# Attention of the second layer with plain fp32 products on half arrays, two heads at a time, in a two-layer diffusion backbone on one Trainium2 core

## The chip, the cores and the metric

The kernel runs on one core of a Trainium2 chip. The metric is device time in microseconds for one execution, and the figure quoted is the median of several. PE is the matrix engine TensorE (PEld its weight loads), DVE is VectorE, ACT is ScalarE, POOL is GpSimd and SP is the queue that issues the loads from memory.

## The reference, cut to what matters

The model has two layers over 256 latent tokens (x) and 256 context tokens (c), width 1024. Each layer is a feed-forward network, a token mixer, and a second feed-forward network, each behind a modulated RMS norm. The first layer mixes with latent attention. The second, the last one, mixes with windowed attention (SWA): 16 query heads of 64 in 4 groups, one key and value head per group, and a sink logit per head. Only the latent stream has an output, so only latent queries are needed.

```
q_x, k_x, v_x = project(hx);  q_c, k_c, v_c = project(hc)      # 16 q heads, 4 k and v heads, of 64
q_x_rot, k_x_rot = apply_rope(q_x), apply_rope(k_x)
s_w = where(|kpos - qpos| <= 128, q_rot . k_rot, NEG) * scale  # latent keys: rotated
s_c = q_plain . k_c * scale                                    # context keys: not rotated
p_w, p_c = softmax over [s_w, s_c, sink logit]
out = (p_w . v_x + p_c . v_c) @ w_o
```

## The kernel before

Activations lie transposed: a tile has 128 features in its partitions and 512 columns, 256 latent (X) and 256 context (C). Almost every product is made by `mm3`: both operands are split into a high part (fp32r) and a low part (what is left), and three fp32r matmuls add high·high, high·low and low·high into a bank of PSUM (lines L210, L211 and L212). `split` makes the parts: a cast on ACT (L182) and a subtraction on DVE or POOL (L183). Weights are loaded by SP, 128x1024 at a time, and split in the same way into `whi` and `wlo`.

The order of the instructions on each engine is fixed when the program is built, by a scheduler that may move independent work; the rows under "The change" show that order. Tiles come from rings: 8 banks of PSUM, 46 `r2k` tiles (128x512), 7 `strip`, 6 `tmp`, 4 `big`, 4 `whi` and 4 `wlo`. A new tile waits until the last reader of the one it replaces is done.

`swa` is the function that changes. It works on 8 pairs of heads, m = 0 to 7; here a pair is two neighbouring heads of one group, 128 features of the query projection. Its steps are these:

- `project(m)` multiplies the normed input by a 128-column block of the query weights (24 matmuls). The plain query goes to two tiles, one for each head: `stack` puts the high part of the head's 64 rows in one half of the partitions and the low part in the other half (a cast on ACT, L515, and a subtraction on DVE or POOL, L516, of 64 partitions each). So a product over all 128 partitions takes in high and low of one head at once.
- `rope(m)` rotates: a matmul with a permutation `perm` swaps halves (L497), DVE multiplies by sine and cosine (L499, L501), POOL adds (L502), and `stack` splits the result again, with the subtractions on POOL.
- `keys` and `doubled` do the like for the keys: their high part stands in both halves of one tile and their low part in both halves of another (L521 to L524), for each of the 4 groups.
- `scores(m)` makes four banks, two heads by two blocks of 128 queries, each 128 x 512 keys: four fp32r matmuls of 256 columns (L763 to L766) and one bf16 matmul that adds the mask band (L768).
- `softmax` takes each bank: maximum on DVE (L451, L455), exponential with sum on ACT (L457), then sink and reciprocal (L463, L464, L466) and scaling on DVE (L471) or ACT (L469).
- `turn` transposes the weights (16 transposes on PE, L479) into four banks, each of which `split` turns into two tiles.
- `apply(m)` multiplies by the values: 24 matmuls (8 `mm3` terms) into one bank. The values lie in `big` tiles with zeros between the groups' 64 columns, so that each head adds zeros to the other's 64 output rows. Then a `split`.

`pipeline` runs the steps in rounds: turn(h), project(h+4), scores(h+2), rope(h+3), apply(h). Below, the round of h is the time from the start of turn(h) to the start of turn(h+1) on PE. Ahead of round 0 stand keys, values and the first projections and scores; behind round 7 `closing` multiplies by the output weights `swo`, whose splits the scheduler places partly inside the rounds. The bank ring is passed 11 times a round: four for turn, one for project, four for scores, one for rope and one for apply.

Of the kernel before, what the change touches and what calls it, by code (L numbers as in the profile page):

```python
# [17 lines left out]
P = 128  # L18
# [19 lines left out]
def hybrid_backbone_kernel(ctx, tc, t, out):  # L38
# [9 lines left out]
    def r2k(n=512, parts=P):  # L48
        return ring.tile([parts, n], F32R, tag="r2k", name="r2k", bufs=46)
# [7 lines left out]
    def big():  # L57
        return ring.tile([P, 1152], F32R, tag="big", name="big", bufs=4)
# [120 lines left out]
    def split(hi, lo, src, bias=None, engine=nc.vector):  # L179

        if bias is None:
            nc.scalar.copy(hi, src)  # L182
            return engine.tensor_tensor(lo, src, hi.bitcast(F32), ALU.subtract)  # L183
# [326 lines left out]

    def stack(dst, R, half, engine=nc.vector):

        a = slice(64 * half, 64 * half + 64)
        b = slice(64 - 64 * half, 128 - 64 * half)
        nc.scalar.copy(dst[a], R[a])  # L515
        return engine.tensor_tensor(dst[b], R[a], dst[a].bitcast(F32), ALU.subtract)  # L516
# [189 lines left out]


    def swa(sl, nxt):
        l, hs = sl.l, sl.hs
        K, V, W = [None] * 4, [], {}  # L710
# [23 lines left out]
        ropes = {}  # L734

        def project(m):
            if m < len(sl.lead):
                o = sl.lead[m][1]
            else:
                wt = weight(t["swq"][m], engine=nc.vector if m == 2 else nc.gpsimd)  # L740
                o = bank()
                mm3(o[:, :T], sl.terms(wt, P, X))
            qs = [r2k(), r2k()]
            for i, q in enumerate(qs):
                stack(q[:, C], o[:, :T], i)
            ropes[m] = StackedRope(o[:, :T], [q[:, C] for q in qs]), qs
            return qs

        def rope(m):
            R = strip()  # L750
            rp, qs = ropes.pop(m)
            rp.into(R)
            for i, q in enumerate(qs):
                stack(q[:, X], R, i, nc.gpsimd)

        def scores(m, *qs):
            k = K[m // 2]
            os = []
            for half, q in enumerate(qs):
                for i in range(2):  # L760
                    o = bank()
                    qx, qc = q[:, i * P:(i + 1) * P], q[:, T + i * P:T + (i + 1) * P]
                    nc.tensor.matmul(o[:, X], lhsT=qx, rhs=k[0][:, X], start=True, stop=False)  # L763
                    nc.tensor.matmul(o[:, X], lhsT=qx, rhs=k[1][:, X], start=False, stop=False)
                    nc.tensor.matmul(o[:, C], lhsT=qc, rhs=k[0][:, C], start=False, stop=False)
                    nc.tensor.matmul(o[:, C], lhsT=qc, rhs=k[1][:, C], start=False, stop=False)  # L766
                    far = slice((1 - i) * P, (2 - i) * P)
                    nc.tensor.matmul(o[:, far], lhsT=ident16, rhs=band[:, i, :], start=False, stop=True)  # L768
                    os.append((o, TT))
# [3 lines left out]
            return softmax(os, SWA_SCALE, place, sink[:, heads], minus_sink[:, heads])  # L773

        def turn(*es):
            return [transposed(es[2 * half:2 * half + 2], k0) for half in range(2) for k0 in (0, 2)]
# [12 lines left out]
        kx = [keys(m, 0) for m in range(2)]  # L789
        kropes = [Rope(o) for o in kx]  # L790
        values(0, 2)
        Rs = [tmp() for _ in range(2)]
        for R, rp in zip(Rs, kropes):
            rp.into(R[:, X])
        rope(0)
        rope(1)
        for m, R in enumerate(Rs):
            nc.scalar.copy(R[:, C], keys(m, 1))
        for m, R in enumerate(Rs):
            for i in range(2):  # L800
                kk = (r2k(), r2k())
                doubled(*kk, R, i)
                K[2 * m + i] = kk
# [110 lines left out]
def _layout(x, c, ctx, c_ctx, mod_w, mod_b, norm_g, final_norm_g, ffn_w_in, ffn_w_out, mla_w_down, mla_q_norm,  # L914
# [36 lines left out]
    put("swq", tiles(swa_w_qkv[0][:, :1024], P).reshape(8, P, 1024))  # L951
    put("swk", tiles(swa_w_qkv[0][:, 1024:1280], P).reshape(2, P, 1024))
    put("swv", swa_w_qkv[0][:, 1280:].reshape(2, 4, P, 256).transpose(0, 2, 1, 3).reshape(2, P, 1024))
    put("swo", tiles(swa_w_o[0], P).reshape(KT, P, 1024))
    put("sink", np.broadcast_to(swa_sink[0][None, :], (P, 16)))
# [34 lines left out]
```

## Time and profile before

| what | value |
|---|---|
| median of 3 runs | 1734.75 us (1734.36 to 1736.54) |
| the profiled execution | 1734.44 us, its span 1732.5 us |
| instructions in the span | 24034 |
| PE busy | 1682.6 us (97%) |
| DVE busy | 1065.3 us (61%) |
| ACT busy | 666.9 us (38%) |
| POOL busy | 185.2 us (11%) |
| scores(0) starts on PE | 1400.43 us |
| turn(1) starts | 1433.17 us |
| turn(5) starts | 1477.89 us |

The profiled execution's own time is 1.9 us above its span, and 0.3 us below the median. Busy times of PE are generous, since matmuls overlap in the pipeline and their ends are modelled: two matmuls of 280 ns that start 120 ns apart each count until they end. So the text works with the distances between starts. All times of day are microseconds from the span's start.

### The profile page before, as it was taken

To read this page: it belongs to the slowest core of one execution; us is meant where nothing else is said; L and a number is where in the kernel's file an instruction comes from. 1 tells how busy PE (TensorE), PEld (TensorE's weight loads), DVE (VectorE), ACT (ScalarE), POOL (GpSimd) and SP (SyncE) were. 2 spreads that over 40 slices of the span, in tenths; PEclk is the share of its full clock that TensorE was granted. 3 is DMA by queue.
4 is the path that set the end of the run, shared out by engine and by line. 5 is a ranking of instruction groups with operands and counts; after the bars stand their busy time and mean duration, and the time that the engine had idled before them with its cause. 6 is when DMAs were issued, how large, how long until landed. Compare 5 with 4: busy or idle time off the path is not lost.

```text
span 1732.5 us, 24034 instructions
## 1 busy us (share of the span) xinstructions
PE 1682.6 (97%) x9512; PEld 1440.9 (83%) x9512; DVE 1065.3 (61%) x1592; ACT 666.9 (38%) x1135; POOL 185.2 (11%) x183
## 2 busy tenths in 40 slices
PE   7999999999999999999999999999999988989997
PEld 4688888888788898888888898888888888889997
DVE  4877576645667567856946374635433589755554
ACT  4322222225556352222222352222222577554443
POOL 1000000004132130000000220000000452110001
PEclk9999999999999999999999999999999999999998
DMA  8566355431212136644645254634222221145553
GB/s 331 187 199 195 129 188 189 147 125 64 86 49 72 51 98 203 198 147 156 219 126 172 93 173 160 215 121 161 94 98 92 93 85 46 53 148 182 173 191 99
DMA packets 72831, 242.71 MB, mean 140 GB/s; under 512 B 8848, under 2 KB 10640, under 8 KB 72720
## 3 DMA queue, kind: packets, MB, share of 16 engines
q1 hardware_dynamic: 72720, 241.20, 42.3%
q8 instruction: 74, 1.21, 0.3%
q14 instruction: 37, 0.30, 0.1%
HBM read 240.11 MB, written 1.05 MB: 139 GB/s over the span
## 4 chain that ended last, share of the span: by engine, by line
PE 87%; DVE 5%; issue 2%; ACT 2%; POOL 1%; DMA 1%; SPq 0%; POOLq 0%; ACTq 0%; DVEq 0%
PE bank L210 28%; PE bank L211 28%; PE bank L212 28%; DVE r2k L183 1%; DVE small L451 1%; PE bank L157 1%; DVE wlo L183 1%; DMA r2k<-in_modo 1%; PE bank L479 1%; PE bank L223 0%; POOL wlo L183 0%; PE bank L102 0%; DMA big<-in_win 0%; DVE r2k L294 0%; ACT r2k L182 0%
## 5 line engine op out<-in xcount | busy, mean ns | idle before, releaser
L210 PE MATMUL bank<-r2k,whi 128*128 128x512 f32 (+1 forms) x2610 | 915.2, 352 | 4.0 <-ACT r2k L185 2.4
L212 PE MATMUL bank<-r2k,wlo 128*128 128x512 f32 (+1 forms) x2610 | 911.8, 350 | 4.3 <-POOL wlo L183 2.2
L211 PE MATMUL bank<-r2k,whi 128*128 128x512 f32 (+1 forms) x2610 | 912.4, 350 | 3.1 <-DVE r2k L186 1.2
L182 ACT CAST whi<-wraw 128x1024 fp32r<-128x1024 f32 (+1 forms) x313 | 321.7, 1028 | 885.7 <-PE bank L211 521.8
L210 PEld LDWEIGHTS bank<-r2k,whi 128*128 128x128 f32 x2610 | 493.5, 190 | 83.1 <-ACT whi L182 9.2
L212 PEld LDWEIGHTS bank<-r2k,wlo 128*128 128x128 f32 x2610 | 494.7, 190 | 69.6 <-POOL wlo L183 3.1
L211 PEld LDWEIGHTS bank<-r2k,whi 128*128 128x128 f32 x2610 | 495.0, 190 | 68.2 <-DVE r2k L186 1.9
L183 DVE TENSOR_TENSOR wlo<-wraw,whi 128x1024 fp32r<-128x1024 f32 (+1 forms) x302 | 363.1, 1204 | 138.9 <-ACT whi L182 131.9
L151 DVE SCALAR_TENSOR_TENSOR big<-modraw,conds,big 128x1024 f32<-128x1024 f32 x196 | 242.3, 1279 | 13.1 <-DMA modraw<-in_modw 12.1
L364 DVE SCALAR_TENSOR_TENSOR x<-bank,mod,x 128x256 f32<-128x256 f32 x192 | 86.1, 479 | 180.4 <-PE bank L212 180.4
L248 POOL TENSOR_TENSOR strip<-strip 128x256 f32<-128x256 f32 x64 | 65.7, 1041 | 1116.5 <-ACT strip L242 765.5
L425 DVE TENSOR_TENSOR tmp<-bank,tmp 128x512 f32<-128x512 f32 (+1 forms) x88 | 54.9, 624 | 179.6 <-PE bank L212 177.7
L183 DVE TENSOR_TENSOR r2k<-bank,r2k 128x512 fp32r<-128x512 f32 (+2 forms) x107 | 62.1, 616 | 18.9 <-ACT r2k L182 18.5
L182 ACT CAST r2k<-bank 128x512 fp32r<-128x512 f32 (+2 forms) x107 | 52.4, 542 | 16.8 <-PE bank L212 16.0
L183 DVE TENSOR_TENSOR r2k<-tmp,r2k 128x512 fp32r<-128x512 f32 (+1 forms) x88 | 54.4, 618 | 1.5 <-ACT r2k L182 1.4
L182 ACT CAST r2k<-tmp 128x512 fp32r<-128x512 f32 (+1 forms) x88 | 49.7, 566 | 10.1 <-DVE tmp L425 9.8
L423 ACT ACTIVATE tmp<-bank 128x512 f32<-128x512 f32 (+1 forms) x88 | 47.3, 537 | 6.8 <-PE bank L212 6.7
L451 DVE TENSOR_REDUCE small<-bank 128x1 f32<-128x512 f32 (+1 forms) x64 | 37.7, 613 | 0.3 <-PE bank L652 0.2
L242 ACT ACTIVATE strip<-x 128x256 f32<-128x256 f32 x80 | 30.6, 410 | 17.8 <-DVE x L364 17.0
L186 DVE SCALAR_TENSOR_TENSOR r2k<-r2k,mod 128x256 fp32r<-128x256 f32 x45 | 28.3, 652 | 8.4 <-ACT r2k L185 7.8
L457 ACT ACTIVATE tmp<-bank,small 128x512 f32<-128x512 f32 x32 | 21.8, 687 | 18.4 <-DVE small L453 14.6
L104 DVE TENSOR_TENSOR mod<-bank,c_modb 128x4 f32<-128x4 f32 x56 | 5.2, 153 | 36.9 <-PE bank L102 36.9
(158 smaller groups left out, 1072.5 us busy)
## 6 DMA issues: line engine op xcount, KB each, us to landing
wraw<-in_win SPq DMA_DIRECT2D x172, 512.0 KB, 3.5
modraw<-in_modw SPq DMA_DIRECT2D x128, 512.0 KB, 4.2
wraw<-in_wout SPq DMA_DIRECT2D x64, 448.0 KB, 3.3
wraw<-in_wout SPq DMA_DIRECT2D x32, 512.0 KB, 3.6
r2k<-in_modo SPq DMA_DIRECT2D x32, 256.0 KB, 5.8
wraw<-in_mwo SPq DMA_DIRECT2D x8, 512.0 KB, 3.5
wraw<-in_swq SPq DMA_DIRECT2D x8, 512.0 KB, 3.5
wraw<-in_swo SPq DMA_DIRECT2D x8, 512.0 KB, 3.4
```

Of the source, the lines that this page charges most:

```text
L151: nc.vector.scalar_tensor_tensor(acc[s], raw, conds[:, kt, s:s + 1], acc[s], ALU.mult, ALU.add)
L182: nc.scalar.copy(hi, src)
L183: return engine.tensor_tensor(lo, src, hi.bitcast(F32), ALU.subtract)
L210: nc.tensor.matmul(o, lhsT=ah, rhs=bh, start=(i == 0), stop=False)
L211: nc.tensor.matmul(o, lhsT=ah, rhs=bl, start=False, stop=False)
L212: nc.tensor.matmul(o, lhsT=al, rhs=bh, start=False, stop=(i == n - 1))
L242: nc.scalar.activation(q, x, AF.Square)
L248: nc.gpsimd.tensor_tensor(self.parts[0], self.parts[0], q, ALU.add)
L364: nc.vector.scalar_tensor_tensor(xs[d][:, SL[s]], o[:, SL[s]], mod[l][:, s, c:c + 1], xs[d][:, SL[s]], ALU.mult, ALU.add)
L423: nc.scalar.activation(sg[:, :w], og[:, :w], AF.Silu)
L425: nc.vector.tensor_tensor(pr[:, :w], ou[:, :w], sg[:, :w], ALU.mult)
L451: nc.vector.tensor_reduce(top[:, j:j + 1], o[:, :w], axis=AX.X, op=ALU.max)
```

## The change

Queries, keys and values are no longer split in `swa`. They are kept as plain fp32, and scores, the swap of the rotation and the products with the values are plain fp32 matmuls (which the profile records as two each). Heads are paired across neighbouring groups: `order` permutes the query weights, the output weights and the sinks on the host, so that pair m holds one head of group 2(m//4) and one of group 2(m//4)+1. Their keys lie in the lower and the upper 64 partitions of one tile K[m//4].

- `scores` multiplies 64 partitions at a time: head h takes rows 64h to 64h+63 of the array, and the two heads alternate, into different banks. The four mask matmuls follow at the end.
- `apply` writes 64 partitions at a time: head h takes columns 64h to 64h+63 of the array, all 128 rows, into the two halves of one bank.
- `project`, the keys, the values and `turn` end in one copy each (on ACT, or on DVE for every second bank of `turn`) in place of splits.
- `roped` uses one fp32 matmul, one multiplication on POOL, one on DVE and the addition on POOL, straight into the query or key tile.
- `doubled`, the stacking, the zeroed `big` tiles and their memsets are gone.

The projections, the output product, the softmax and the transposes on PE are as before; the order of the banks inside a pair is now by query block first.

```diff
         def values(t0, t1):
...
-                v = big().rearrange("p (i c) -> p i c", i=2)
-                nc.gpsimd.memset(v.bitcast(F32), 0.0)
-                inner = v[:, :, 64:].rearrange("p i (g d) -> p i g d", d=P)[:, :, :, :64]
-                split(inner[:, 0], inner[:, 1], o[:, :T].rearrange("p (g d) -> p g d", g=4))
+                v = r2k(T).bitcast(F32)
+                nc.scalar.copy(v, o[:, :T])
...
+        def roped(dst, plain):
+            sw = bank()[:, :T]
+            nc.tensor.matmul(sw, lhsT=perm[:, 0].bitcast(F32), rhs=plain, start=True, stop=True)
+            u, v = strip(), strip()
+            nc.gpsimd.tensor_tensor(v, plain, ropeC, ALU.mult)
+            nc.vector.tensor_tensor(u, sw, ropeS, ALU.mult)
+            nc.gpsimd.tensor_tensor(dst, u, v, ALU.add)
...
         def project(m):
...
-            qs = [r2k(), r2k()]
-            for i, q in enumerate(qs):
-                stack(q[:, C], o[:, :T], i)
+            q = r2k().bitcast(F32)
+            nc.scalar.copy(q[:, C], o[:, :T])
...
+        def scores(m, q):
+            k = K[m // 4]
+            os = {(h, i): bank() for i in range(2) for h in range(2)}
+            for i in range(2):
+                for s in range(2):
+                    for h in range(2):
+                        nc.tensor.matmul(os[h, i][:, SL[s]], lhsT=q[half(h), s * T + i * P:s * T + (i + 1) * P], rhs=k[half(h), SL[s]],
+                                         start=(s == 0), stop=False)
+            for i in range(2):
+                far = slice((1 - i) * P, (2 - i) * P)
+                for h in range(2):
+                    nc.tensor.matmul(os[h, i][:, far], lhsT=ident16, rhs=band[:, i, :], start=False, stop=True)
...
         def turn(*es):
...
+                    p = r2k().bitcast(F32)
+                    if k0:
+                        nc.vector.tensor_copy(p, b)
+                    else:
+                        nc.scalar.copy(p, b)
...
         def apply(m, *pts):
             o = bank()
-            c0 = P * (m // 2) + 64
-            mm3(o[:, :T], [((V[kt][:, 0, c0 - 64 * half:][:, :P], V[kt][:, 1, c0 - 64 * half:][:, :P]),
-                            pair(pts[2 * half + kt // 2], slice(None), slice(kt % 2 * T, kt % 2 * T + T)))
-                           for half in range(2) for kt in range(4)])
+            for kt in range(4):
+                for h in range(2):
+                    nc.tensor.matmul(o[half(h), :T], lhsT=V[kt][:, half(m // 4 * 2 + h)], rhs=pts[2 * h + kt // 2][:, SL[kt % 2]],
+                                     start=(kt == 0), stop=(kt == 3), skip_group_check=True)
...
+        plain = []
+        for m in range(2):
+            p = tmp(T)
+            nc.scalar.copy(p, keys(m, 0))
+            plain.append(p)
         values(0, 2)
+        for m in range(2):
+            K[m] = r2k().bitcast(F32)
+            roped(K[m][:, X], plain[m])
...
+    order = [h for m in range(2) for g in range(4) for h in (8 * m + g, 8 * m + 4 + g)]
```

The order on PE around scores(0), where it stood and where it stands. The lines of `scores` are L763 to L768 before and L769 and L774 now; `band` and `ident` are the mask and the unit matrix.

```order
L763 MATMUL bank<-r2k 128x256
L764 MATMUL bank<-r2k 128x256
L765 MATMUL bank<-r2k 128x256
L766 MATMUL bank<-r2k 128x256
L768 LDWEIGHTS ident_633
L768 MATMUL bank<-band_631,ident_633 128x128
```

```order
+L769 MATMUL bank<-r2k 128x256 [waits Pool_49]
+L769 MATMUL bank<-r2k 128x256
+L769 MATMUL bank<-r2k 128x256 [waits Activation_49]
+L769 MATMUL bank<-r2k 128x256 x5
+L774 LDWEIGHTS ident_633
+L774 MATMUL bank<-band_631,ident_633 128x128
```

The first piece stood four times in a row, one bank each. Now eight products over 64 partitions come first, for all four banks, and the four masks after them, so that the four banks become complete together.

The order on DVE inside a round: before, from the scaling of one softmax (L471) through the splits of turn's four banks (L183 of 128x512) into the maxima of the next (L451) and the query's stacking (L516).

```order
L464 TENSOR_TENSOR small<-small 128x2
L466 RECIPROCAL small<-small 128x2
L471 TENSOR_SCALAR x<-x,small 128x2x256
L183 TENSOR_TENSOR r2k<-bank,r2k 128x512 x3
L451 TENSOR_REDUCE small<-bank 128x1 x2
L183 TENSOR_TENSOR r2k<-bank,r2k 128x512
L516 TENSOR_TENSOR r2k<-bank,r2k 64x256
L455 TENSOR_SCALAR small<-small,minus_sink 128x1 x2
L451 TENSOR_REDUCE small<-bank 128x1
L516 TENSOR_TENSOR r2k<-bank,r2k 64x256
L455 TENSOR_SCALAR small<-small,minus_sink 128x1
L451 TENSOR_REDUCE small<-bank 128x1
```

The same place now; L790 is the copy of one bank of turn, L742 the sine product of the rotation.

```order
L471 TENSOR_SCALAR tmp<-tmp,small 128x512
L790 COPY r2k<-bank 128x512
L464 TENSOR_TENSOR small<-small 128x2
L790 COPY r2k<-bank 128x512
L466 RECIPROCAL small<-small 128x2
L471 TENSOR_SCALAR tmp<-tmp,small 128x512
L183 TENSOR_TENSOR wlo<-wraw,whi 128x1024
L451 TENSOR_REDUCE small<-bank 128x1 x2
L455 TENSOR_SCALAR small<-small,minus_sink 128x1 x2
L451 TENSOR_REDUCE small<-bank 128x1 x2
L455 TENSOR_SCALAR small<-small,minus_sink 128x1 x2
L742 TENSOR_TENSOR strip<-bank,c_ropeS 128x256
```

The four splits have become two copies, which now stand between the two scalings of a softmax instead of behind them; the two stackings are gone, and the four maxima stand together.

More of the change, by code (lines that the diff above doesn't have):

```diff
@@ L709, in swa, with half @@
         l, hs = sl.l, sl.hs
-        K, V, W = [None] * 4, [], {}
+        K, V, W = [None] * 2, [], {}
+        def half(i):
+            return slice(64 * i, 64 * i + 64)
         def keys(m, s):
@@ L742, in project @@
                 mm3(o[:, :T], sl.terms(wt, P, X))
-            qs = [r2k(), r2k()]
-            for i, q in enumerate(qs):
-                stack(q[:, C], o[:, :T], i)
-            ropes[m] = StackedRope(o[:, :T], [q[:, C] for q in qs]), qs
-            return qs
-        def rope(m):
[L750 to L769, printed above, removed]
@@ L770, in scores @@
             heads = slice(2 * m, 2 * m + 2)
             place = (lambda j: tmp()) if m % 2 else (lambda j: x_all[:, 2 * j:2 * j + 2, C])
-            return softmax(os, SWA_SCALE, place, sink[:, heads], minus_sink[:, heads])
+            return softmax([(os[h, i], TT) for h in range(2) for i in range(2)], SWA_SCALE, place, sink[:, heads], minus_sink[:, heads])
         def turn(*es):
-            return [transposed(es[2 * half:2 * half + 2], k0) for half in range(2) for k0 in (0, 2)]
+            pts = []
@@ new lines, in turn @@
+            for h in range(2):
+                for k0 in (0, 2):
+                    b = bank()
+                    for kk in range(2):
+                        for i in range(2):
+                            nc.tensor.transpose(b[:, kk * T + i * P: kk * T + (i + 1) * P], block(es[2 * h + i], k0 + kk), ident)
+                    p = r2k().bitcast(F32)
[3 more added lines that the diff above has]
+                        nc.scalar.copy(p, b)
+                    pts.append(p)
@@ L788, in swa @@
         q = [project(0), project(1)]
-        kx = [keys(m, 0) for m in range(2)]
-        kropes = [Rope(o) for o in kx]
+        plain = []
[3 more added lines that the diff above has]
+            plain.append(p)
         values(0, 2)
-        Rs = [tmp() for _ in range(2)]
-        for R, rp in zip(Rs, kropes):
-            rp.into(R[:, X])
+        for m in range(2):
+            K[m] = r2k().bitcast(F32)
+            roped(K[m][:, X], plain[m])
         rope(0)
         rope(1)
[L797 to L803, printed above, removed]
+        for m in range(2):
+            nc.scalar.copy(K[m][:, C], keys(m, 1))
         q.append(project(2))
@@ L950, in _layout @@
     put("mwo", tiles(mla_w_o[0], P).reshape(KT, P, 1024))
-    put("swq", tiles(swa_w_qkv[0][:, :1024], P).reshape(8, P, 1024))
+    order = [h for m in range(2) for g in range(4) for h in (8 * m + g, 8 * m + 4 + g)]
+    put("swq", tiles(swa_w_qkv[0][:, :1024].reshape(D, 16, 64)[:, order].reshape(D, D), P).reshape(8, P, 1024))
     put("swk", tiles(swa_w_qkv[0][:, 1024:1280], P).reshape(2, P, 1024))
     put("swv", swa_w_qkv[0][:, 1280:].reshape(2, 4, P, 256).transpose(0, 2, 1, 3).reshape(2, P, 1024))
-    put("swo", tiles(swa_w_o[0], P).reshape(KT, P, 1024))
-    put("sink", np.broadcast_to(swa_sink[0][None, :], (P, 16)))
+    put("swo", tiles(swa_w_o[0].reshape(16, 64, D)[order].reshape(D, D), P).reshape(KT, P, 1024))
+    put("sink", np.broadcast_to(swa_sink[0][order][None, :], (P, 16)))
     pos = np.arange(T)
```

8 lines of the change are left out of this document (7 added, 1 removed).

## The prediction

> **What bounds the kernel now.** I read the page first, then the stretches of the second layer's attention, then one round engine by engine.
>
> ```profile
> PE 1682.6 (97%) x9512; PEld 1440.9 (83%) x9512; DVE 1065.3 (61%) x1592; ACT 666.9 (38%) x1135; POOL 185.2 (11%) x183
> PE 87%; DVE 5%; issue 2%; ACT 2%; POOL 1%; DMA 1%; SPq 0%; POOLq 0%; ACTq 0%; DVEq 0%
> ```
>
> Over the whole span PE bounds, and the chain lies on PE for 87%. That is a mean over stages. The change touches only 1383 to 1499 us, so the stretches there decide:
>
> ```profile
> core 0: us, PE busy (x) PEld busy (x) DVE busy (x) ACT busy (x) POOL busy (x), PEclk, DMA share, GB/s
> 1383.47:1400.43 16.96, 14.93 (x118) 14.13 (x117) 13.24 (x25) 10.50 (x25) 8.99 (x11) 1.00 0.18 63
> 1400.43:1415.82 15.39, 14.33 (x116) 13.52 (x115) 13.48 (x28) 12.15 (x25) 6.96 (x3) 1.00 0.20 69
> 1415.82:1433.17 17.35, 13.87 (x87) 12.71 (x87) 13.92 (x32) 12.86 (x32) 8.54 (x7) 0.80 0.28 92
> 1433.17:1444.17 11.00, 10.37 (x88) 10.01 (x87) 10.17 (x22) 9.09 (x22) 1.54 (x2) 1.00 0.15 48
> 1444.17:1455.92 11.75, 10.38 (x88) 10.02 (x87) 11.30 (x26) 9.15 (x23) 2.27 (x3) 1.00 0.15 47
> 1455.92:1467.66 11.74, 10.36 (x88) 10.00 (x87) 11.30 (x26) 9.16 (x23) 2.27 (x3) 1.00 0.14 46
> 1467.66:1477.89 10.23, 8.15 (x64) 7.31 (x63) 10.15 (x24) 7.12 (x18) 2.25 (x3) 1.00 0.17 51
> 1477.89:1498.81 20.92, 17.96 (x147) 16.94 (x146) 15.97 (x37) 14.91 (x37) 2.46 (x3) 1.00 0.00 1
> ```
>
> The rows from 1433.17 on are rounds 1, 2, 3, 4 and then the tail (rounds 5 to 7). In rounds 2 and 3 DVE is busy 11.30 of 11.75 us; PE has 10.38 and waits for the rest. So here DVE sets the round and PE is a close second. The chain of waits over the rounds says the same, and one round on PE shows where the wait falls:
>
> ```profile
> by line: DVE r2k L183 16.4%; DVE small L451 15.7%; issue 8.3%; DVE wlo L183 7.0%; DVE small L464 6.4%; ACT r2k L182 4.9%; DVE x L471 4.9%; ACT tmp L469 4.0%; DVE small L455 3.8%; DVE r2k L516 3.5%; ACT tmp L457 3.4%; DVE tmp L471 3.2%; PE b
> ```
>
> ```profile
> 1444.17 1.91 PE L479 MATMUL bank<-c_ident,x 128*128 128x128 f32 x16
> ...
> 1445.84 0.36 PE L210 MATMUL bank<-r2k,whi 128*128 128x256 f32 x1
> ...
> 1448.80 0.28 PE L763 MATMUL bank<-r2k 128*128 128x256 f32 x1
> ...
> 1451.12 0.48 PE L497 MATMUL bank<-r2k,permr 128*128 128x256 f32 x2
> 1452.97 0.36 PE L210 MATMUL bank<-r2k,big 128*128 128x256 f32 x1 [1.37 <-DVE r2k L183]
> ...
> 1455.92 0.27 PE L479 MATMUL bank<-c_ident,tmp 128*128 128x128 f32 x1
> ```
>
> From start to start: turn 1.67, project 2.96 (24 matmuls, 0.123 each), scores 2.32, rope 0.48, a wait of 1.37 for DVE's split of the transposes, apply 2.95. So PE's own work is 10.38 a round.
>
> **The change, part by part: PE.** The price of a plain fp32 matmul is in the norm at the kernel's start (L824) and in the column sums of the modulation (L157), which run on four quarters of the columns:
>
> ```profile
> 11.88 3.17 PE L824 MATMUL bank<-tmp,ones 128*128 128x512 f32 x7
> 14.46 0.59 PE L824 MATMUL bank<-tmp,ones 128*128 128x512 f32 x1
> ...
> 83.12 0.39 PE L212 MATMUL bank<-r2k,wlo 128*128 128x512 f32 x1
> 83.44 1.06 PE L157 MATMUL bank<-big,ones 128*32 128x512 f32 x8
> 84.43 0.50 PE L210 MATMUL bank<-r2k,whi 128*128 128x512 f32 x1
> 84.77 0.40 PE L211 MATMUL bank<-r2k,whi 128*128 128x512 f32 x1
> ```
>
> L824: starts are (14.46 - 11.88) / 6 = 0.43 apart for 512 columns, so 0.214 for 256, and there are two records to a matmul. L157: eight records would take 8 x 0.43 = 3.4 one after another, and took 1.06: four column tiles ran side by side. The full-array stream around them starts every 0.23, but took 0.32 into the tiles, started again where L157 had 0.07 left instead of 0.16, and needed 0.34 for its first step: some 0.29 for one visit to tiles and back.
>
> - apply: 24 matmuls go (2.95), 8 come, 16 records, two column halves at a time: 16 x 0.214 / 2 = 1.71, plus a visit of 0.29: 2.0. Gain 0.95. Bounds 1.71 (no visit cost) and 3.42 + 0.29 (no overlap); L157 is the very form, so I take 2.0.
> - scores: 16 products go and 8 come, 1.71 likewise plus 0.29, and four masks in a row, which took at most 0.12 each between the products; I take 0.3. Together 2.3 against 2.32: nothing. No row shows halves of the rows side by side. Bounds 1.71 + 0.3 and 3.42 + 0.59; nearest is L157, another split of the same array, so I take overlap. Each record needs its own weights of 128 columns, and the loads alone follow one another every (0.98 - 0.19) / 7 = 0.11 here, so 16 loads (1.8) just fit:
>
> ```profile
> 1371.58 0.98 PEld L223 LDWEIGHTS bank<-ones,strip 128*128 128x128 f32 x8
> ```
>
> - rope: two records of 0.214 for two of 0.24: 0.45 for 0.48. turn and project stay.
>
> A round on PE becomes 1.67 + 2.96 + 2.3 + 0.45 + 2.0 = 9.4.
>
> The Trainium skill, "TensorE: Matmul & The Clock Gate", section "Measured speedup vs the span model", gives 3.07x for four row tiles and 2.38x for three column tiles, about 0.78 of the ideal; this trace has 3.4 us of records in 1.06 with their latency, so for columns it beats that, and for rows no run here shows it. By the page a visit's 1.71 would be an estimated 2.2 and the time about 1723.
>
> **DVE, ACT and POOL.** Rows of round 2 (1444.17 to 1455.92), then POOL's over the whole stage:
>
> ```profile
> L183 DVE TENSOR_TENSOR r2k<-bank,r2k 128x512 fp32r<-128x512 f32 x4 | 2.6, 683 | 0.2 <-ACT r2k L182 0.2
> L183 DVE TENSOR_TENSOR wlo<-wraw,whi 128x1024 fp32r<-128x1024 f32 x1 | 1.5, 1457 | 0.0
> L516 DVE TENSOR_TENSOR r2k<-bank,r2k 64x256 fp32r<-64x256 f32 x2 | 0.8, 422 | 0.1
> L501 DVE TENSOR_TENSOR strip<-bank,c_ropeC 128x256 f32<-128x256 f32 x1 | 0.4, 411 | 0.0
> ```
>
> ```profile
> L182 ACT CAST r2k<-bank 128x512 fp32r<-128x512 f32 x4 | 2.2, 586 | 0.0
> L515 ACT CAST r2k<-strip 64x256 fp32r<-64x256 f32 x2 | 0.8, 398 | 0.0
> L515 ACT CAST r2k<-bank 64x256 fp32r<-64x256 f32 x2 | 0.7, 368 | 1.4 <-DVE r2k L516 1.4
> ```
>
> ```profile
> L516 POOL TENSOR_TENSOR r2k<-strip,r2k 64x256 fp32r<-64x256 f32 x16 | 13.6, 848 | 8.9 <-ACT r2k L515 8.3
> L183 POOL TENSOR_TENSOR wlo<-wraw,whi 128x1024 fp32r<-128x1024 f32 x5 | 12.5, 2514 | 9.7 <-ACT whi L182 7.8 <-PE bank L212 1.1 <-POOL r2k L516 0.8
> L502 POOL TENSOR_TENSOR strip<-strip 128x256 f32<-128x256 f32 x8 | 5.9, 737 | 37.7 <-PE bank L479 23.6 <-DVE small L464 13.6 <-DVE small L466 0.4
> ```
>
> DVE loses the two L516 (0.8), L501 (0.4) and four splits (2.6), and gains two copies of a bank, at most a split each (1.3): 2.5 less, 11.30 - 2.5 = 8.8. ACT loses 1.5 of stacking and two of four casts (1.2) and gains the query's copy (0.4): 9.15 - 2.3 = 6.9. POOL's two L516 (1.7) become one product like L502 (0.74): shorter. Nothing is costed at nothing but what PE's 9.4 covers, and DVE's cover is only 0.6 deep. The loads on SP are the same in number. Copies of turn now stand behind the next softmax's first scaling on DVE; apply, who waits for them, comes after project and scores on PE (5.3 us), so I take no wait.
>
> So PE takes over as the bound of rounds 1 to 3: 3 x 9.4 = 28.2 against 34.5, a gain of 6.3. Round 4 has no project and in the new order no `wlo`: PE 6.4, DVE 8.8 - 1.5 = 7.3; I take 7.4 against 10.23: 2.8.
>
> Round 0 and what leads to it gain most. The first softmax was late because DVE was doubling the keys:
>
> ```profile
> 1402.34 1.88 DVE r2k L522
> ...
> 1404.85 1.92 DVE r2k L524
> ...
> 1407.64 0.70 DVE r2k L522
> ...
> 1413.66 0.49 DVE x L471
> ```
>
> Those three, a second L524 and two L516 put some 5.8 us on the chain from scores(0) to its last scaling at 1413.66, 13.2 after 1400.43; all of them go, so 7.4 remain. PE reaches turn(0) after scores 2.3, values 48 x 0.123 = 5.9, scores 2.3, rope 0.45, project 2.96: 13.9. So turn(0) waits for nothing, and PE runs on with turn 1.67, project 2.96, scores 2.3, rope 0.45 and apply 2.0 to turn(1): 23.3 in place of 32.74 (1400.43 to 1433.17), a gain of 9.4. This includes the clock: the 0.80 in that row is a stretch at half clock after PE's waits, which no longer occur. If it comes back it costs about 0.2 x 17.35 = 3.5.
>
> Ahead of 1400.43 the rotation's waits and the splits on DVE shrink against four fp32 products of 0.43: gain 0.4 (between -1 and 2, PE idles 2.0 there). The tail's 20.92 hold three applies, three turns and one scores, 16.2 us of PE, and waits of 4.7. Now 13.3 of PE; with all waits 18.0, with half of them 15.7; I take a gain of 4.0. Behind the tail everything is as before, only earlier.
>
> Sum: 0.4 + 9.4 + 6.3 + 2.8 + 4.0 = 22.9. Against it I set waits: in round 1, where DVE was not yet full (10.17 of 11.00), PE still idled 0.63. Seven rounds of 0.6 are 4.2. Gain 18.7. The profiled execution took 1734.44 (span 1732.5): 1715.7. The median shown is 0.3 above it: 1716.0.
>
> **The rivals.**
>
> - The halves overlap only in part, or new waits take what the splits give back. POOL's order has two `wlo` splits of 2.51 ahead of the addition for pair 2, which scores(2) needs; if these stay as late as now, PE stands 1 to 2 us there, and DVE's margin of 0.6 is soon gone. With a third of the overlap lost scores and apply take 0.5 more each: some 7 us in all. Time about 1723. For it: DVE at 8.8 against 9.4. Against it: L157.
> - Row halves run one after the other: 1.71 more for each scores. Three ahead of turn(1), three in rounds 1 to 3, 0.7 in round 4 (PE 8.1 over 7.4), one in the tail: 12.6. Gain 6.1, time 1728.6. For it: no row shows the form.
> - Neither kind of half overlaps, so the change does not do what it says: 1.71 more for each apply too, 1.7 + 5.1 + 1.7 + 5.1 = 13.6. Loss 7.5, time 1742, slower. It decides from 1.2 us lost per visit on (18.7 over 16 visits, eight scores and eight applies); L157 speaks against it for columns.
> - The gain is given back behind the tail: no change. The tail's DMA share is 0.00 and its engines wait for arithmetic, so little speaks for it.
>
> **How the numbers follow.** My forecast 0.68 (own range 1709 to 1721), partial overlap or waits 0.15, rows in turn 0.10, no overlap 0.04, given back 0.03. About 0.2% (3.5 us) is what a measurement of this kernel can tell from no change. Faster is the first three, 0.93; same 0.03; slower 0.04. The low end takes no waits (4.2), no cost of visits (16 x 0.29 = 4.6) and the clock kept: 1716.0 - 8.8 is 1707; the high end is rows in turn, 1729.
>
> **What would show it.** Right: the round on PE at 9.4 to 10, records of L769 and L800 two by two at 0.11 mean distance, DVE below 9 a round, no half clock at 1415 to 1433, turn(1) near 1424. Wrong: L769 at 0.21 from start to start; PE waiting for POOL's L743 or for banks ahead of L769; DVE still busy over 95% of a round.

## The result: 1.2% faster, and the profile after

The changed kernel takes 1714.93 us (median of 4, 1713.85 to 1716.32) against 1735.07 for the kernel before, run beside it: 20.1 us less, ratio 0.9883 with a 95% interval of 0.9869 to 0.9898. The forecast was 1716.0. The profiled execution took 1715.96, 1.0 above the median; its span is 1714.2.

The page's line of busy times, as it is now:

```profile
PE 1674.9 (98%) x9448; PEld 1421.5 (83%) x9448; DVE 1029.5 (60%) x1536; ACT 643.9 (38%) x1087; POOL 175.2 (10%) x173
```

The stretches of the second layer's attention: the lead-in, scores(0) to turn(1), rounds 1, 2, 3 and 4, the tail, and then a piece of the tail (columns as in the prediction):

```profile
1385.24:1401.32 16.08, 15.02 (x118) 14.47 (x116) 7.76 (x10) 6.39 (x17) 9.72 (x12) 1.00 0.20 66
1401.32:1424.22 22.90, 22.90 (x193) 20.04 (x192) 14.42 (x34) 16.04 (x36) 13.93 (x9) 1.00 0.33 108
1424.22:1434.13 9.91, 9.82 (x80) 7.60 (x79) 7.78 (x23) 6.92 (x17) 1.47 (x2) 1.00 0.24 77
1434.13:1443.73 9.60, 9.60 (x80) 7.62 (x79) 7.47 (x21) 6.92 (x17) 1.47 (x2) 1.00 0.17 59
1443.73:1453.32 9.59, 9.59 (x81) 7.62 (x79) 7.45 (x21) 6.92 (x17) 1.47 (x2) 1.00 0.16 54
1453.32:1460.70 7.38, 6.80 (x56) 4.71 (x55) 6.75 (x20) 6.23 (x16) 0.73 (x1) 1.00 0.18 65
1460.70:1479.88 19.18, 16.42 (x118) 11.86 (x116) 11.94 (x34) 12.46 (x33) 0.73 (x1) 0.91 0.00 1
...
1474.00:1476.00 2.00, 2.00 (x9) 0.86 (x6) 0.00 (x0) 0.16 (x1) 0.00 (x0) 0.50 0.00 0
```

The bound of the rounds has changed hands: PE is busy 9.60 of 9.60, DVE 7.5. But the column for the clock shows a new half-clock stretch, in the tail (0.50 in the last row). Round 2 on PE without its project, and the tail from turn(6) on:

```profile
1434.13 2.18 PE L787 MATMUL bank<-c_ident,x 128*128 128x128 f32 x16
...
1439.11 2.00 PE L769 MATMUL bank<-r2k 64*128 64x256 f32 x16
1441.04 0.40 PE L774 MATMUL bank<-band,ident 128*128 128x128 bf16 x4
1441.27 0.65 PE L739 MATMUL bank<-r2k,permr 128*128 128x256 f32 x2
1441.85 1.95 PE L800 MATMUL bank<-r2k 128*64 128x256 f32 x16
...
1467.11 1.97 PE L787 MATMUL bank<-c_ident,x 128*128 128x128 f32 x16
1471.58 0.65 PE L800 MATMUL bank<-r2k 128*64 128x256 f32 x2 [2.51 <-ACT r2k L792]
1472.15 0.33 PE L787 MATMUL bank<-c_ident,tmp 128*128 128x128 f32 x1
1472.41 3.39 PE L800 MATMUL bank<-r2k 128*64 128x256 f32 x14
```

Sixteen records of the scores take 2.00: less the 0.39 of the last one, that is 0.107 from start to start. Apply's take 1.95. So both kinds of halves run side by side, without loss. Turn's row takes 2.18, where turn's row before (1444.17 in the prediction) took 1.91: it now waits some 0.26 between its transposes. In the tail, apply(6) waits 2.51 for ACT's copy of the transposes, and its 14 records then need 3.39 where 16 needed 1.95.

One thing must be taken out before stages are compared. This execution was already late when the attention began. The column sums, which the prediction shows at 83.44, stand here:

```profile
85.19 1.06 PE L157 MATMUL bank<-big,ones 128*32 128x512 f32 x8
```

That is 1.75 later, long before any edited line. In the profiles of the other kernels below the same row stands up to 0.3 earlier or about 2 later than at 83.44, so it is the start of a single execution, not the change. Counted from that row on:

| stage | before | now | gain | predicted gain |
|---|---|---|---|---|
| column sums to scores(0) | 1316.99 | 1316.13 | 0.9 | 0.4 |
| scores(0) to turn(1) | 32.74 | 22.90 | 9.8 | 9.4 |
| rounds 1 to 3 | 34.49 | 29.10 | 5.4 | 6.3 |
| round 4 | 10.23 | 7.38 | 2.9 | 2.8 |
| tail (turn(5) to the closing) | 20.92 | 19.18 | 1.7 | 4.0 |
| behind the tail | 233.69 | 234.32 | -0.6 | 0 |
| sum | | | 20.1 | 22.9, less 4.2 of waits |

The last two stages belong together. Before, five matmuls of the closing product stood inside the tail (1495.46 to 1495.94, 0.12 apart); now none does. So 0.6 of the tail's gain is work that moved behind it, which is the 0.6 lost there. The tail itself gained 1.1.

### The profile page after: what moved, and what is told of

It reads as the page before. It is cut to its first block, busy times and chain, and to the rows that moved or that the text cites. A ratio compares the mean times of both kernels' runs of the same rounds, so it can differ in the third digit from the quotient of the medians.

```text
span 1714.2 us, 23757 instructions
## 1 busy us (share of the span) xinstructions
PE 1674.9 (98%) x9448; PEld 1421.5 (83%) x9448; DVE 1029.5 (60%) x1536; ACT 643.9 (38%) x1087; POOL 175.2 (10%) x173
## 3 DMA queue, kind: packets, MB, share of 16 engines
HBM read 240.11 MB, written 1.05 MB: 141 GB/s over the span
## 4 chain that ended last, share of the span: by engine, by line
PE 90%; DVE 3%; ACT 3%; DMA 2%; issue 2%; POOL 1%; SPq 0%; POOLq 0%; ACTq 0%; DVEq 0%
PE bank L210 28%; PE bank L211 28%; PE bank L212 28%; DMA r2k<-in_modo 1%; PE bank L157 1%; DVE wlo L183 1%; DVE small L451 0%; PE bank L479 0%; ACT whi L182 0%; PE bank L223 0%; PE bank L102 0%; PE bank L800 0%; ACT tmp L457 0%; DVE r2k L294 0%; DMA big<-in_win 0%
## 5 line engine op out<-in xcount | busy, mean ns | idle before, releaser
L183 DVE TENSOR_TENSOR wlo<-wraw,whi 128x1024 fp32r<-128x1024 f32 (+1 forms) x302 | 363.6, 1206 | 145.5 <-ACT whi L182 138.8
L183 DVE TENSOR_TENSOR r2k<-tmp,r2k 128x512 fp32r<-128x512 f32 (+1 forms) x88 | 54.4, 618 | 1.5 <-ACT r2k L182 1.4
L183 DVE TENSOR_TENSOR r2k<-bank,r2k 128x512 fp32r<-128x512 f32 (+2 forms) x73 | 40.7, 593 | 17.5 <-ACT r2k L182 17.1
L451 DVE TENSOR_REDUCE small<-bank 128x1 f32<-128x512 f32 (+1 forms) x64 | 37.0, 614 | 7.4 <-PE bank L774 7.2
L182 ACT CAST r2k<-bank 128x512 fp32r<-128x512 f32 (+2 forms) x73 | 34.4, 524 | 14.2 <-PE bank L212 8.8
```

What stands on the lines that cost most here:

```text
L451: nc.vector.tensor_reduce(top[:, j:j + 1], o[:, :w], axis=AX.X, op=ALU.max)
```

## The experiments

Times are medians. The changed kernel stands at 1714.93 throughout; the kernel before, run beside each of these, took 1734.9 to 1735.5.

### Do the halves run side by side?

**Rows head by head.** The same instructions in another order:

```diff
-            for i in range(2):
-                for s in range(2):
-                    for h in range(2):
+            for h in range(2):
+                for i in range(2):
+                    for s in range(2):
                         nc.tensor.matmul(os[h, i][:, SL[s]], ...
```

> The scores' products in the order head, block, stream: the eight records of one half of the rows come one after the other, then the eight of the other half; same instructions. Theory (two halves run side by side when neighbouring records lie on different halves): from start to start 0.108 becomes 0.214, a scores grows by 15 x 0.107 = 1.6, eight of them by 12.8, nearly all on PE's path: some 12 us slower than the changed kernel, about 1727. Rival (the records come at 0.108 whatever their neighbour is, since the weight loads at 0.11 set the pace): no change, 1715.

1718.45: 3.5 slower, not 12. PE's row for the scores, then the records of that line in three stretches of it (busy time and, in brackets, records that run in the stretch):

```profile
1440.96 2.96 PE L769 MATMUL bank<-r2k 64*128 64x256 f32 x16
...
1440.95:1441.92 0.97, 0.96 (x4) 1.00 0.00 0
1441.92:1442.79 0.87, 0.87 (x9) 1.00 0.00 0
1442.79:1443.70 0.91, 0.91 (x7) 1.00 0.00 0
...
1436.20:1446.55 10.35, 10.35 (x81) 8.50 (x79) 7.54 (x20) 7.04 (x18) 1.46 (x2) 1.00 0.16 53
1464.39:1482.19 17.80, 15.64 (x118) 11.68 (x117) 11.64 (x33) 12.06 (x31) 0.73 (x1) 1.00 0.00 1
```

The first half starts alone, four records in 0.97. Then both run together, and the second ends alone. The second head did not wait for the first: it started beside the first one's fifth record, with three of the first still to come. (The rows don't name the half. But on one half alone records stand 0.22 apart, as the run without a second half shows, so two that start together lie on different halves.) So the order costs 0.96 a scores, not 1.6. The rounds took 10.35, only 0.75 more, and the tail (the last row) became 1.4 shorter, with its clock at 1.00. Both theories were too simple: neighbours matter, but PE looks some records ahead.

**Columns head by head.** The same swap of loops in `apply`.

```diff
-            for kt in range(4):
-                for h in range(2):
+            for h in range(2):
+                for kt in range(4):
                     nc.tensor.matmul(o[half(h), :T], lhsT=V[kt]...
```

> Apply's products in the order head, tile of keys: the eight records of one half of the columns, then those of the other; same instructions. Theory (side by side only as neighbours): 0.105 becomes 0.214, 1.6 for each of eight applies, all on PE's path: about 1727. Rival (pace set by the loads): 1715.

1716.36: 1.4 slower, not 12. The look-ahead again: an apply takes 0.91 more, not 1.6. And again the tail (17.64) kept its clock, and its 1.5 gave back most of the 1.8 that rounds 1 to 3 lost (10.29 for 9.60 in round 2):

```profile
1442.17 2.86 PE L800 MATMUL bank<-r2k 128*64 128x256 f32 x16
...
1462.69:1480.33 17.64, 16.39 (x117) 12.07 (x116) 10.69 (x29) 11.46 (x28) 0.73 (x1) 1.00 0.00 1
```

**No second half at all.** This prices the prediction's rival "rows in turn" without the look-ahead. The second head's own scores are left out.

```diff
-  lhsT=q[half(h), s * T + i * P:...], rhs=k[half(h), SL[s]]
+  lhsT=q[half(0), s * T + i * P:...], rhs=k[half(0), SL[s]]
```

> Both heads of a pair take their query and key from the lower half of the rows (the second head's own scores are left out), so all sixteen records of a scores lie on one half: no overlap is possible. Theory: 0.214 from start to start, 3.2 for 1.62, so 1.6 a scores, more than the 0.97 that the order head by head cost (there the last four records of one half ran beside the first four of the other). Of it 4.8 ahead of turn(1), 1.3 in each of rounds 1 to 3 after turn's wait of 0.26 is used up, 0.7 in round 4, and the tail 0.8 shorter, since its half clock goes as in that run: about 9 slower than the changed kernel, 1723.5. Rival (what the prediction gave for rows in turn): 12.6 slower, 1727.5. Second rival (the pace is set by weight loads): 1715.

1725.26: 10.3 slower. The scores' records now stand 0.223 apart ((3.72 - 0.38) / 15), 1.7 more for each scores, the round is 1.5 longer, scores(0) to turn(1) 5.2 longer, and the tail 0.6 shorter:

```profile
1443.26 3.72 PE L769 MATMUL bank<-r2k 64*128 64x256 f32 x16
...
1399.32:1427.38 28.06, 28.06 (x193) 24.39 (x192) 15.77 (x38) 16.95 (x39) 13.82 (x9) 1.00 0.33 104
1427.38:1438.50 11.12, 11.12 (x81) 9.10 (x79) 7.54 (x20) 7.04 (x18) 1.46 (x2) 1.00 0.21 71
```

So side by side running of the rows alone is worth 10 of the 20 us, and the number of weight loads, which is the same, does not set the pace.

**What a visit to the halves costs.** Two masks are moved in behind the second product and two behind the sixth; the block of four masks at the end goes.

```diff
                 for s in range(2):
                     for h in range(2):
                         nc.tensor.matmul(os[h, i][:, SL[s]], ...)
+                    if s == 0:
...
+                        for h in range(2):
+                            nc.tensor.matmul(os[h, i][:, far], lhsT=ident16, rhs=band[:, i, :], ...)
...
```

> The four masks of a scores stand between the products, two behind the second and two behind the sixth, so PE goes to the halves three times instead of once. Theory (a visit costs 0.29: 0.09 into the halves and 0.2 out of them, as the changed kernel's starts show): 0.6 a scores, 4.8 in all, less the 0.26 a round that turn waits anyway and the 0.57 of round 4: 2 to 3.5 slower than the changed kernel, 1717 to 1718.5. Rival (the masks slip in beside the other half's records): no change, 1715.

1718.68: 3.8 slower, just over the expected span.

```profile
1440.59 0.70 PE L769 MATMUL bank<-r2k 64*128 64x256 f32 x4
1441.22 0.28 PE L774 MATMUL bank<-band,ident 128*128 128x128 bf16 x2
1441.44 1.13 PE L769 MATMUL bank<-r2k 64*128 64x256 f32 x8
1442.51 0.28 PE L774 MATMUL bank<-band,ident 128*128 128x128 bf16 x2
1442.72 0.70 PE L769 MATMUL bank<-r2k 64*128 64x256 f32 x4
1443.35 0.70 PE L739 MATMUL bank<-r2k,permr 128*128 128x256 f32 x2
```

From the first product to the rotation it is now 2.76, against 2.16 before the move: 0.30 for each of the two visits more. The prediction's 0.29 was right. The Trainium skill, "TensorEngine Tiling (Array Packing)", section "Key Properties", says that a change of the tiling mode drains the array; the 0.30 a visit agree with it, though no row shows the drain itself.

### Which engine held the rounds?

**Apply as before, the rest as changed.** Values, `turn` and `apply` go back to splits and 24 matmuls.

```diff
-  nc.tensor.matmul(o[half(h), :T], lhsT=V[kt][:, half(...)], rhs=pts[...], ...)   # 8
+  mm3(o[:, :T], [((V[kt][:, 0, c0[h]:][:, :P], V[kt][:, 1, ...]), pair(pts[...], ...)) ...])   # 24
```

> One part alone: scores, keys and queries as changed; values, turn and apply as before (24 matmuls on split values, four splits a round). Theory (PE bounds the rounds and each term counts by itself): apply 2.95 for 1.88, PE 9.6 + 1.1 = 10.7 a round, DVE 7.5 + 1.3 = 8.8 stays under it. Three rounds 3.3, round 4 1.1, ahead of turn(1) 1.1, the tail 3 x 1.1 and some waits for the longer splits: 9 to 10 slower than the changed kernel, about 1724.5. Rival (what counts is DVE's relief, PE's terms are hidden): DVE is still under PE, so at most 2 us slower, 1717.

1723.16: 8.2 slower, somewhat less than expected. Rounds 2 and 3 are 10.23 and 10.24, not 10.7, with PE busy throughout and DVE at 9.0, so PE sets them:

```profile
1445.92:1456.16 10.24, 10.24 (x89) 9.56 (x87) 9.08 (x22) 7.84 (x20) 2.24 (x2) 1.00 0.18 57
```

From start to start apply takes 1.18 more (3.06 for 1.88), but the rotation ahead of it 0.28 less (0.30 for 0.58), since no halves follow, and turn's wait of 0.26 is gone. What is left is the round's 0.64. Rounds 1 to 3 make only 1.9 of the 8.2; some 3.5 are the tail's, with a wait of 2.84 and a half clock of its own.

**DVE filled again, PE as changed.**

```diff
-                    if k0:
-                        nc.vector.tensor_copy(p, b)
-                    else:
-                        nc.scalar.copy(p, b)
+                    nc.vector.tensor_copy(p, b)
+                    nc.vector.tensor_copy(p, b)
```

> The changed kernel with DVE filled again: each of turn's four banks is copied twice by DVE, none by ACT: DVE 7.5 + 6 x 0.68 = 11.5 a round, PE 9.6 as it is. Theory (the round is the larger of the two, so both had to fall): rounds 1 to 3 at 11.5 to 12, +6 to +7; round 4 10.8 for 7.4, +3.5; the start and the tail +2 to +4: about 1728. Rival (PE's fewer matmuls alone carry the gain, DVE's queue has room): at most 2 us slower, 1717.

1729.88: 15.0 slower. Three quarters of the gain are gone, though PE's work is that of the changed kernel. Round 3, and the tail:

```profile
1447.41:1458.25 10.84, 10.46 (x80) 7.77 (x79) 10.84 (x26) 5.96 (x15) 1.47 (x2) 1.00 0.16 53
...
1468.29:1496.11 27.82, 19.75 (x132) 13.81 (x132) 22.16 (x53) 9.36 (x25) 0.73 (x1) 0.94 0.00 1
```

DVE is busy 10.84 of 10.84: the round is the larger of the two engines. But rounds 1 to 3 lost 4.3, not the 6 to 7 expected, and round 4 2.7. The tail lost 8.6, where apply waits three times for DVE's chain (1.33, 3.21 and 2.81) and the clock falls once. So the 15.0 are not the price of full rounds alone.

**The before kernel with DVE relieved.** The low parts of `turn`'s splits are not made; `apply` takes the high part twice.

```diff
-            return [transposed(es[2 * half:2 * half + 2], k0) for half in range(2) for k0 in (0, 2)]
+                    hi = r2k()          # after the same 16 transposes
+                    nc.scalar.copy(hi, b)
+                    out.append((hi, hi))
```

> The kernel before without the low parts of turn's splits: the first part is used twice (the low part is left out), so four DVE operations of 0.68 a round go and PE's instructions stay. DVE 11.3 - 2.6 = 8.7, PE 10.4 as before. Theory (DVE alone is what holds the rounds of before at 11.7, and without it PE's 10.4 does): rounds 1 to 3 at 10.4 to 10.6 (3.1 less together), round 4 some 1.8 less, the tail 3 less: 8 faster than before, about 1727. Rival (relief of DVE is worth nothing as long as PE keeps its matmuls): 1733 or more.

1727.07: 8.4 faster than the kernel before, as expected, but not where it was expected. Rounds 1 and 2 came near PE's own time (10.72, 10.93); rounds 3 and 4 came to 11.75 and 11.60. In round 4 a wait for POOL, which subtracts in the query's stacking (L516), took the place of the one for DVE, and brought the half clock with it:

```profile
1429.02:1439.74 10.72, 10.50 (x88) 10.00 (x87) 7.87 (x20) 8.92 (x23) 3.60 (x3) 1.00 0.14 52
1462.42:1474.02 11.60, 9.08 (x65) 8.51 (x64) 8.76 (x25) 9.76 (x28) 3.92 (x5) 0.85 0.12 45
...
1466.86 0.39 PE L763 MATMUL bank<-r2k 128*128 128x256 f32 x1 [2.52 <-POOL r2k L516]
```

What made up the sum was scores(0) to turn(1), 4.6 less, and the tail, 4.3 less. So with DVE relieved the next wait is for the stacking on POOL. That the stacking had to go too is read from this wait; no run takes it out alone. (In round 3, turn waited 1.0 in two pieces, for ACT and for DVE's part of the rotation.)

**The before kernel with one key tile doubled instead of four.** All heads use the one.

```diff
+                if m or i:
+                    K[2 * m + i] = K[0]
+                    continue
                 kk = (r2k(), r2k())
                 doubled(*kk, R, i)
```

> The kernel before, but only the first of the four doubled key tiles is made and all heads use it (the other three are left out): six of the eight operations of the doubling on DVE go, 5.8 us or so; PE's instructions are the same. Theory (the start's gain of 9.8 came from DVE's late first softmax and the half clock behind it, not from PE's fewer matmuls): scores(0) to turn(1), 32.7, falls to 25 or 26, the rounds stay at 11.7: 1727 to 1729. Rival (the gain there is PE's own): at most 1 us faster, 1734.

1728.61: 6.7 faster than the kernel before. Scores(0) to turn(1) fell from 32.74 to 25.39, at full clock and with the same matmuls:

```profile
1402.27:1427.66 25.39, 24.26 (x203) 23.42 (x202) 19.41 (x51) 21.42 (x50) 14.20 (x8) 1.00 0.30 105
```

So 7.4 of the 9.8 gained at the start were DVE's doubling and the half clock that PE's waits brought. The other 2.5 are PE's cheaper steps and the 1.1 of waits that this kernel still has (25.39 less 24.26).

### Where the tail's gain went

**PE kept busy in the wait.** Twenty transposes into a bank that nothing reads, behind the last of turn(6).

```diff
...
+            if len(turns) == 7:
+                warm = bank()
+                with behind(last):
+                    for _ in range(20):
+                        nc.tensor.transpose(warm[:, :P], ident, ident)
```

> Twenty transposes of the unit matrix into a bank that nothing reads fill 2.2 of the 2.51 us in which PE waits ahead of apply(6); the copies stay where they are. Theory (the idle time brings the half clock): no 0.50 after the wait, apply(6) at 0.105 instead of 0.212, the tail 1.4 to 1.7 shorter, about 1713.4. Rival (the clock falls there for another reason, or the half clock costs nothing since softmax(7) ends later anyway): 1715.

1714.13. The ranges overlap (1713.75 to 1714.83), so the tail of the profiled execution decides: 17.31 for 19.18.

```profile
1468.46 2.35 PE L801 MATMUL bank<-c_ident 128*128 128x128 f32 x20
1471.13 2.43 PE L808 MATMUL bank<-r2k 128*64 128x256 f32 x16 [0.32 <-ACT r2k L795]
...
1471.13:1477.56 6.43, 6.43 (x48) 4.57 (x49) 2.63 (x6) 2.70 (x5) 0.00 (x0) 1.00 0.00 0
```

The copies came when they had come before, but the clock stayed at 1.00, and from apply(6) to the closing it took 6.43 for 8.30. Some of the 1.87 is a stray transpose in the middle of apply(6) that went too (the row at 1472.15 above); the rest is the half clock.

**The copies ahead of the exponentials.** turn(6)'s four copies get priority in the scheduler:

```diff
...
+                    with tc.high_priority() if len(turns) == 7 else nullcontext():
                         if k0:
                             nc.vector.tensor_copy(p, b)
                         else:
                             nc.scalar.copy(p, b)
```

> Only the order on ACT and DVE in the tail: turn(6)'s copies get priority and stand ahead of the last exponential and the scalings of softmax(7). Theory (apply(6) waits 2.51 for copies that stand behind the exponentials on ACT, and this wait brings the half clock of 0.50 at 1474 to 1476): the wait falls to about 1.1, the clock stays at 1.00, the tail of 19.2 becomes 16 to 17: 1712.3. Rival (the softmax(7) chain sets the end, and is later by what the copies take): tail as before, 1715.

1712.10 (1710.60 to 1712.77), ratio to the kernel before 0.9867 (0.9851 to 0.9883): 2.8 faster than the changed kernel, with no overlap of the ranges (the two ratios' intervals still overlap in part), and the best version of this study. The tail shows the same 2.8:

```profile
1468.18 0.65 PE L804 MATMUL bank<-r2k 128*64 128x256 f32 x2 [1.05 <-ACT r2k L796]
...
1458.77:1475.13 16.36, 15.06 (x119) 10.84 (x117) 12.03 (x34) 12.25 (x33) 0.72 (x1) 1.00 0.00 1
```

**Two attempts on top of that failed.** First, the four banks of a scores were taken in the softmax's order against a wait of 0.26 for turn's last bank that is left in rounds 2 and 3.

```diff
-            os = {(h, i): bank() for i in range(2) for h in range(2)}
+            os = {(h, i): bank() for h in range(2) for i in range(2)}
```

> The kernel with the tail's new order, and besides the four banks of a scores are taken in the order in which the softmax reads them. Theory (turn's last bank waits 0.26 a round, 0.6 in round 1, for a bank that the softmax frees late): 1 to 1.5 faster than 1712.1, about 1710.8. Rival (turn waits for the softmax of the bank itself, or the new order frees another late one): 1712 or slower.

1712.57, the round 9.61 as before: the wait is not a matter of that order, and which reader it waits for stays open. Second, apply was put ahead of scores in rounds 0 to 3, in `pipeline`.

```diff
+            if early and h < 4:
+                rope(h + 3)
+                apply(h, *p)
             if h + 2 < n:
                 e.append(scores(h + 2, *q.pop(0)))
...
```

> The kernel with the tail's new order, and in rounds 0 to 3 apply stands directly ahead of scores on PE, behind the rotation, so that halves of the columns go over into halves of the rows without full-array work between. Theory (the 0.29 is paid at the border to the full array alone): 0.3 a round, four rounds, 1.2 faster than 1712.1, about 1710.9. Rival (going from columns to rows drains the array too, or the scores, now 2 us later, make the next softmax late and turn waits): 1712 or slower.

1714.76. Round 0 shows the clean order:

```profile
1419.61 1.95 PE L808 MATMUL bank<-r2k 128*64 128x256 f32 x16
1421.49 2.00 PE L773 MATMUL bank<-r2k 64*128 64x256 f32 x16
```

Apply's start to scores' start is 1.88 (1421.49 - 1419.61), exactly what it is to a full-array step (1441.85 to 1443.73 in the changed kernel). So going from columns to rows costs as much as going to the full array. In rounds 1 to 3 the scheduler also put two records of the scores into apply (at 1439.75, behind two of apply's), and each such pair pays for two changes more: the round became 10.4.

## Why the prediction was right, step by step

- **Halves side by side**, the step it rested on: right at full size. 0.107 and 0.105 between starts for the forecast 0.11, 0.30 a visit for 0.29. The third of the overlap that the first rival lost did not go. The Trainium skill, "TensorE: Matmul & The Clock Gate", section "Measured speedup vs the span model", gives 3.07x for four row tiles, 0.77 of the ideal; for two halves this trace has all of it (0.107 side by side, 0.223 on one half).
- **PE's round of 9.4**: rounds 2 and 3 are 9.60, of which 0.26 are a wait of turn, so its own work is 9.34.
- **DVE 8.8 a round**: too high by 1.3; it is 7.5. The operations that I counted came out as counted. What I missed is that others became shorter: two kinds by 1.0 (last section), and the weights' split from 1457 to 1226 ns. It cost nothing, as PE bounds.
- **Start 9.4**: 9.8. The mechanism (doubling, late softmax, half clock) is shown by the run with one key tile. turn(0) waited for nothing.
- **Rounds 1 to 3, 6.3 before waits**: 5.4, since waits of 1.1 came and PE's own work was 0.2 less; net 0.9. **Round 4**: 7.38 for 7.4, with a wait of 0.57 for POOL's addition (L743). With one of 0.25 in the tail for the same addition, that is all that came of the rival on POOL's order.
- **The tail, 4.0**: the term that was mis-sized; it gave 1.7, and 1.1 without the closing's five matmuls. Its 19.18 lies above even my "all waits kept", 18.0. I had counted PE's work and the old waits, but not that a shorter apply leaves PE waiting longer in one piece behind ACT's queue (2.51), and that a half clock follows. The run with a busy PE and the one with early copies show both parts.
- **The 4.2 set against it for waits**: 0.9 in the rounds, none in round 4 and 2.3 in the tail came, 3.2 in all. With 0.5 more at the lead-in, 0.4 more at the start and 0.6 for the closing's five matmuls, the gain is 20.1 for 18.7. That the sum came so near is partly luck: the 4.2 was set for 0.6 in each of seven rounds, and most of what it had to cover was a loss in the tail that I had not foreseen.
- **Rival "rows in turn"**: priced at 12.6, measured 10.3. A longer round first uses up turn's 0.26, and the tail happened to keep its clock, which left it 0.6 shorter.

## What to carry to other kernels

When products fill only half of the rows or columns, pair two of them on opposite halves, issue them alternately, and put all of them into one visit, since each visit costs 0.3. When two engines are close to the bound, price the change on both and on the helper behind them: with one relieved the wait moved to POOL here. After such a change read the end of the pipeline anew, for one wait in one piece can cost twice, first itself and then the clock.

## What the runs showed of the hardware

- **The look-ahead.** A matmul on one half started 0.97 after the first of eight on the other half, ahead of three that stand before it in the program. So the order of issue matters less than it seems, though not nothing: 0.96 and 0.91 a step.
- **Idle time brings the half clock, but the length of one idle time does not decide.** In the tails, idle times of PE of 1.05, 1.25 and 2.16 left the clock at 1.00 (early copies; columns, rows head by head), and 2.51 and 3.02 brought 0.50 for 3.4 us (the changed kernel; the visits). A line between 2.16 and 2.51 suggests itself, but the next two rows are against it. Behind the first, in the kernel before, 0.50 was granted from 1426.30 to 1433.10; behind the second, in the run with DVE filled, the clock stayed at 1.00:

```profile
1424.96 0.36 PE L763 MATMUL bank<-r2k 128*128 128x256 f32 x1 [1.99 <-DVE r2k L183]
...
1491.22 0.62 PE L798 MATMUL bank<-r2k 128*64 128x256 f32 x2 [2.81 <-DVE r2k L790]
```

Within a trace the clock changes at whole multiples of 3.41 us from one another. The 1.99 lies in one such step; of the 2.81 no step holds more than 1.75. So it may count how much of a step is idle, and then a tail's clock is in part the chance of a single execution. This is not shown, and not the whole rule: ahead of 1704.84 in the changed kernel a step with 1.54 of idle time was followed by 0.50 too.
- **DVE waits for POOL.** Views of round 2 before the change, POOL's rows and DVE's, and then two groups of DVE's in round 2 after it:

```profile
1446.59 0.73 POOL L516 TENSOR_TENSOR r2k<-strip,r2k 64x256 fp32r<-64x256 f32 x1 [1.02 <-ACT r2k L515]
...
1447.39 0.81 POOL L516 TENSOR_TENSOR r2k<-strip,r2k 64x256 fp32r<-64x256 f32 x1
...
1446.57 1.03 DVE L471 TENSOR_SCALAR tmp<-tmp,small 128x512 f32<-128x512 f32 x1
1447.52 0.70 DVE L464 TENSOR_TENSOR small<-small 128x2 f32<-128x2 f32 x1
1448.45 0.49 DVE L471 TENSOR_SCALAR tmp<-tmp,small 128x512 f32<-128x512 f32 x1
...
L471 DVE TENSOR_SCALAR tmp<-tmp,small 128x512 f32<-128x512 f32 x2 | 1.0, 506 | 0.1
L464 DVE TENSOR_TENSOR small<-small 128x2 f32<-128x2 f32 x2 | 0.3, 156 | 0.5 <-ACT small L463 0.5
```

An addition of two columns took 0.70 in place of 0.16 and ended at 1448.22, where POOL ended at 1448.20; the same scaling took 1.03 beside POOL and 0.49 after it. The scalings (L471) between 1424 and 1460 us show the pattern in all fourteen traces, of both kernels and the twelve runs. The 50 that met no POOL operation took 0.48 to 0.49. The 40 that started while one ran, or up to 0.02 ahead of it, ended 0.28 to 0.29 after it. The 8 that started 0.07 or more ahead of one took 0.48 to 0.49 all the same. With POOL's stacking gone, these two kinds alone give DVE 1.0 back a round. The Trainium skill, "SBUF — State Buffer", section "SBUF: two separate sides", says that DVE and GpSimd share one pair of ports under a lock that is held for a whole instruction; these times agree with it.
